# First block's experts: two DRAM accumulators instead of one for the rows that the experts add

## The chip, the cores and the metric

The kernel runs on one core of a Trainium2 chip. The metric is device time in microseconds (us) of one execution. The engines are called PE (TensorE), DVE (VectorE), ACT (ScalarE), POOL (GpSimd) and SP (SyncE); SP computes nothing here and issues the large loads. ACT and POOL issue transfers too, in their own order of work.

## What is computed

Two transformer blocks, one after the other, on 512 tokens of 1024 features. The change lies in the first block's mixture of experts. Each token goes to 8 of 64 experts; its rows are multiplied by a weight and summed, and a shared expert that every token passes is added:

```python
xb = jnp.concatenate([xt, jnp.zeros((1, d), xt.dtype)])[slot_tok].reshape(n_blocks, EXPERT_BLOCK, d)
def expert_block(args):
    xe, e = args
    return (jax.nn.silu(xe @ w_gate_l[e]) * (xe @ w_up_l[e])) @ w_down_l[e]
yb = lax.map(expert_block, (xb, block_e)).reshape(n_slots, d)
routed = jax.ops.segment_sum(yb * slot_w[:, None].astype(yb.dtype), slot_tok, num_segments=t + 1)[:t]
shared = (jax.nn.silu(xt @ w_sh_gate_l) * (xt @ w_sh_up_l)) @ w_sh_down_l
return (routed + shared).reshape(b, l, d)
```

The caller then does `x = x + g2 * _rmsnorm(_moe(h2, *moe_p), norm_ffn_post[i])`, and that `x` is the second block's input.

## The kernel before

`phase_b` holds the first block's expert stage. It works on **blocks**: one block is up to 128 rows (tokens) of one expert. There are 65 blocks of routed experts (128 rows for the first ones, then large and small ones in turn, and at the end of 72 and 64 rows), and ahead of them 4 blocks of the shared expert, one for each 128 tokens. For a routed block the steps are:

- **Gather** (`ex_gather`): POOL issues an indirect DMA that fetches the block's token rows from `h2d` in DRAM into one of four buffers `xg`. So the gather of block b must wait until PE has transposed block b-4.
- **Transpose and two products** (`ex_T`, `ex_gu`): PE transposes `xg`; DVE and ACT copy the result to `xT`; PE multiplies by the gate and up weights (`w`, `wu`); ACT and DVE make `eh`.
- **Down product** (`ex_hT`, `ex_down`): PE multiplies `ehT` by the down weights `wd`; ACT writes the first half of the result `ey`, scaled, and DVE the second half.
- **Scatter** (end of `ex_down`): POOL issues an indirect DMA with an added operation, which adds the rows of `ey` to the rows of `acc`, a [512, 1024] float32 tensor in DRAM. All 65 scatters write the same tensor at places that are known only at run time, so each of them waits on POOL until the one before has landed.

The shared expert's four blocks write `acc` first, as plain DMAs from ACT, and so set its start value.

The weights of an expert are 3 MB: one load `w` of 1 MB and four of 512 KB (`wu`, `wu`, `wd`, `wd`), issued by SP. `wu`, `wd`, `ey`, `xg`, `xT`, the context rows `ct` and the final `ys` are all tiles of 4 KB per partition and share one class of 30 buffers; `u()` hands them out. An instruction that writes such a tile waits for whoever held the buffer before. When that was an `ey`, it waits for a scatter to land.

The code is recorded once, and a scheduler sets each engine's order of instructions. An engine works its list in order: if POOL waits for a landing, the gathers behind wait too.

At the end of the stage stands `overflow()`, a loop whose count is read at run time (for experts that got more rows than planned; it runs no iteration here). All engines meet at its entry and its exit, after all DMAs have landed. Behind it `phase_b` loads `acc` into four tiles `ys` (named `moe` in the trace), and two chains run side by side: PE computes keys and values of the second block's context (`ctx2_kv`, 128 products with `hc`), and `to_mixer` normalizes `ys`, adds it to `x`, normalizes again, and after that PE transposes the result and the second block begins (`hph`, `hpl`). `to_mixer` works on tiles 0 and 1 first, then on 2 and 3.

With 15 blocks to go `ctx2_rows` is started: it loads the context rows `ct` (from ACT), normalizes them (POOL), has PE transpose them and DVE write them to `hc`. Later POOL multiplies a scale `G`.

Of the kernel before, what the change touches and what calls it, by code (L numbers as in the profile page):

```python
# [10 lines left out]
F32 = mybir.dt.float32  # L11
# [10 lines left out]
P = 128  # L22
D = 1024
ND = 8
NX = 512
# [99 lines left out]
class K:  # L125
# [1073 lines left out]
    def phase_b(self):  # L1199
        nc, a, cp, mcol, mT = self.nc, self.a, self.cp, self.mcol, self.mT  # L1200
        self.h2d = self.dp.tile([NX, D], F32, name="h2d")
        self.acc = self.dp.tile([NX, D], F32, name="acc")
        self.x1 = [self.u(D, name="xr") for _ in range(4)]
        for t in range(4):
            nc.scalar.dma_start(self.x1[t], a["x"][t * P:(t + 1) * P])
# [21 lines left out]
        n, nxt, nl = NS + NB, NS + 2, EARLY[0]  # L1227
# [3 lines left out]
        for p in range(n + 1):  # L1231
# [12 lines left out]
            while nl < (EARLY[p] if p < NS else min(NB, b + 1 + AHEAD)):  # L1244
                r, lo, _ = BLOCKS[nl]
# [27 lines left out]
        self.overflow()  # L1273
        wkv += [self.wcols("w_in_2", 1536 + 256 * i, 256) for i in (2, 3)]

        ys = [self.u(D, name="moe") for _ in range(4)]
        for t in range(4):
            nc.sync.dma_start(ys[t], self.acc[t * P:(t + 1) * P])
            self.dump("moe1", ys[t], slice(t * P, t * P + P))
        self.x2 = self.x1  # L1280
        self.hp = []
        self.start(self.to_mixer(ys, G))
# [103 lines left out]
    def route_setup(self):  # L1386
        nc, cp, a = self.nc, self.cp, self.a
        self.wr = self.u(ND, NE, name="wr")
        nc.scalar.dma_start(self.wr, a["w_router"].rearrange("(k p) e -> p k e", p=P))
        shift = self.ps()[:, :NE]  # L1390
        self.acc_mm(shift, [(self.mcol[:, 24 + k:25 + k, 0].to_broadcast([P, P]), self.wr[:, k]) for k in range(ND)])
        self.lsh = self.u(NE, name="lsh1")
        nc.scalar.copy(self.lsh, shift)
        nc.vector.tensor_mul(self.wr, self.wr, self.Af[:, :, None].to_broadcast([P, ND, NE]))
        self.rbias = self.u(NE, name="rbias")
        nc.scalar.dma_start(self.rbias, a["router_bias"].to_broadcast([P, NE]))
        mk = self.mk = self.u(2, P, dt=BF, name="mk")
        nc.vector.tensor_copy(mk[:, 0], self.sq(C_US))
        nc.vector.memset(mk[:, 1], 1.0)
        self.selb = self.u(4, NE, dt=BF, name="selb")  # L1400
        self.pm, self.wts = self.u(4, NE, name="pm"), self.u(4, NE, name="wtsk")

        self.sconst = self.u(4, 3, dt=BF, name="sconst")
        nc.vector.tensor_copy(self.sconst[:, :, 0], self.pos[:, 5:6].to_broadcast([P, 4]))
        for t in range(4):
            nc.vector.memset(self.sconst[:, t, 1:2], float(P * t))
        nc.vector.memset(self.sconst[:, :, 2], 1.0)
        self.aux = self.u(4, NE, 3, dt=BF, name="aux")
        self.iota4 = self.sq(C_IOTA)[:, None, :].to_broadcast([P, 4, P])
        self.cnt = cp.tile([NE, 1], F32, name="cnt")  # L1410
        rr = self.u(2, NE, parts=NE, name="room")
        nc.scalar.dma_start(rr, a["consts"][:NE, O_ROOM:].rearrange("p (r e) -> p r e", r=2))
        self.room, self.rank = rr[:, 0], rr[:, 1]
        self.routed = 0
        self.sorted, self.table = False, {}

    def route(self, t, Ar, Br):
# [131 lines left out]
    def first(self, st):  # L1549

        while self.routed < 4:
            yield
        self.xg = [self.u(D, name="xg") for _ in range(4)]
        for t in range(4):
            self.nc.gpsimd.memset(self.xg[t], 0.0)
        yield from self.slots_steps(0)
        for i in range(2):
            st[NS + i] = self.ex_gather(i)
# [76 lines left out]
    def ex_down(self, s):  # L1635
        nc, c, m = self.nc, s["c"], s["m"]
        y = self.u(D, name="ey")[:c]
        if m == NARROW:
            ps = self.ps()
            for k in range(2):  # L1640
                for j in range(2):
                    nc.tensor.matmul(ps[64 * j:64 * j + 64], s["hT"][:, k], s["wd"][k][:, 512 * j:512 * j + 512],  # L1642
                                     start=(k == 0), stop=(k == 1), tile_position=(0, 64 * j))
            parts = [(ps[64 * j:64 * j + c], s["sw"][64 * j:64 * j + c]) for j in range(2)]
        else:
            parts = []
            for j in range(2):
                ps = self.ps()[:m]
                self.acc_mm(ps, [(s["hT"][:, k], s["wd"][k][:, 512 * j:512 * j + 512]) for k in range(2)])
                parts.append((ps[:c], s["sw"] if "row" in s else s["sw"][:c]))  # L1650
        nc.scalar.activation(y[:, 0:512], parts[0][0], AF.Copy, scale=parts[0][1])
        nc.vector.tensor_scalar(y[:, 512:], parts[1][0], parts[1][1], None, op0=OP.mult)  # L1652
        if "row" in s:
            nc.scalar.dma_start(self.acc[s["row"] * P:(s["row"] + 1) * P], y)
            return
        nc.gpsimd.indirect_dma_start(out=self.acc, out_offset=bass.IndirectOffsetOnAxis(ap=s["idx"][:c], axis=0),  # L1656
                                     in_=y, in_offset=None, bounds_check=NX - 1, oob_is_err=False, compute_op=OP.add)

    def sort_plan(self):
# [699 lines left out]
```

## Time and profile before

| | |
|---|---|
| time, median of 3 runs | 2878.65 us (2872.04 to 2881.9) |
| the profiled execution: its time | 2867.02 us |
| its span, first to last instruction | 2865.2 us |
| mean granted TensorE clock | 0.96 |
| PE busy | 2506.8 us, 87% of the span |
| DVE / ACT / POOL busy | 1064.5 / 541.7 / 588.6 us |
| read and written in DRAM | 748.08 MB and 31.13 MB, 272 GB/s over the span |
| scatters (line 1656 on POOL) | 65, from 797.6 to 1526.7 us |

The times of stages are given as us from the span's start. A busy share says how much an engine worked, not what it was waiting for; for that the rows name in square brackets the idle time ahead of an instruction and what ended it. DMA-issuing instructions on SP and ACT do not count as busy. A DMA's time to landing runs from its issue to its completion.

### The profile page before, as it was taken

What the parts mean: (1) busy time and instruction counts of PE and PEld (TensorE: products, weight loads), DVE (VectorE), ACT (ScalarE), POOL (GpSimd) and SP (SyncE); (2) the same over time, 40 slices, a digit from 0 to 9 for tenths busy, and PEclk for the clock granted to TensorE, in tenths of its full rate; (3) what the DMA queues carried; (4) which work ended last, traced back from release to release, by engine and by line L of the source; (5) the groups of instructions that cost most, each with busy time, mean ns of one, the idle gap of its engine ahead of it and who ended that gap; (6) DMA issues with size and microseconds to landing.
All of it is one profiled execution on the core that took longest, in us unless ns stands there. A gap on an engine that the chain in (4) does not pass through costs nothing. (4 is left out here: it accounts for less than half of the span.)

```text
span 2865.2 us, 36192 instructions
## 1 busy us (share of the span) xinstructions
PE 2506.8 (87%) x13445; PEld 1413.4 (49%) x13445; DVE 1064.5 (37%) x2642; ACT 541.7 (19%) x1129; POOL 588.6 (21%) x438
## 2 busy tenths in 40 slices
PE   6999989998999999887865979969988888888886
PEld 3767869976455443333324858823333333333332
DVE  3673853466434422221213896432111121111122
ACT  4442532122211111111102225300000000000001
POOL 3241343344122112222222652310000000000000
PEclk8999999999999999998987989989999999999998
DMA  7676221145389999999876111389999999999997
GB/s 264 239 267 218 73 82 44 46 144 192 129 309 343 344 342 344 345 332 287 275 221 187 39 60 32 137 312 411 411 411 410 412 412 412 411 411 410 411 411 287
DMA packets 231043, 775.49 MB, mean 271 GB/s; under 512 B 28178, under 2 KB 74450, under 8 KB 207058
## 3 DMA queue, kind: packets, MB, share of 16 engines
q1 hardware_dynamic: 203536, 714.68, 66.0%
q0 software_dynamic: 16288, 37.79, 5.8%
q10 hardware_dynamic: 11042, 20.70, 2.1%
q8 instruction: 107, 1.75, 0.3%
q14 instruction: 70, 0.57, 0.1%
HBM read 748.08 MB, written 31.13 MB: 272 GB/s over the span
## 5 line engine op out<-in xcount | busy, mean ns | idle before, releaser
L2238 PE MATMUL ps<-wu,xT 128*64 128x512 f32 x1448 | 358.6, 596 | 0.1
L2238 PEld LDWEIGHTS ps<-wu,xT 128*64 128x64 f32 x1448 | 129.5, 137 | 210.6 <-issue 185.9
L210 POOL TENSOR_TENSOR wsl<-w,wsh 128x1024 fp32r<-128x1024 f32 x60 | 159.8, 2672 | 236.7 <-ACT wsh L209 192.5
L2293 POOL TENSOR_TENSOR fin<-fin,norm_final_g 128x512 f32<-128x512 f32 x2 | 2.7, 1353 | 984.6 <-ACT fin L2286 984.6
L2244 DVE TENSOR_TENSOR hid<-hid,ps 128x512 f32<-128x512 f32 x32 | 21.4, 687 | 482.7 <-issue 452.7
L2238 PE MATMUL ps<-w,xT 128*64 128x512 f32 x584 | 149.6, 605 | 46.8 <-DMA w<-in_w_up 46.0
L2257 PE MATMUL ps<-wu,hT 128*64 128x512 f32 x752 | 169.1, 594 | 14.1 <-ACT hT L2249 14.1
L1612 PE MATMUL ps<-w,xT 128*128 128x512 f32 (+6 forms) x320 | 153.3, 624 | 27.6 <-DMA w<-in_w_expert 15.3
L1656 POOL DMA_INDIRECT acc<-ey,sidx x65 | 99.0, 1524 | 379.2 <-DMA acc<-ey,sidx 211.9
L1612 PE MATMUL ps<-wu,xT 128*128 128x512 f32 (+6 forms) x320 | 150.4, 610 | 8.4 <-DMA wu<-in_w_expert 4.6
L222 PE MATMUL ps<-wd,ehT 128*128 128x512 f32 (+6 forms) x320 | 145.5, 598 | 1.7 <-DVE ehT L1633 0.9
L1578 POOL DMA_INDIRECT xg<-h2d,sidx x65 | 66.6, 1025 | 234.4 <-PE ps L1642 107.9
L1874 DVE SCALAR_TENSOR_TENSOR cy<-cv,cw,cy 128x512 f32<-128x512 f32 x120 | 114.2, 1013 | 0.4
L1612 PEld LDWEIGHTS ps<-w,xT 128*128 128x128 f32 (+6 forms) x320 | 53.3, 172 | 118.6 <-issue 91.2
L2257 PEld LDWEIGHTS ps<-wu,hT 128*64 128x64 f32 x752 | 53.0, 137 | 116.8 <-issue 93.0
L2238 PEld LDWEIGHTS ps<-w,xT 128*64 128x64 f32 x584 | 43.4, 137 | 136.2 <-issue 68.9
L2243 ACT ACTIVATE hid<-ps 128x512 f32<-128x512 f32 x32 | 18.2, 596 | 481.9 <-PE ps L2238 418.0
L2262 DVE TENSOR_TENSOR y<-ps,G 128x512 f32<-128x512 f32 x16 | 11.1, 692 | 249.0 <-PE ps L2257 249.0
L1612 PEld LDWEIGHTS ps<-wu,xT 128*128 128x128 f32 (+6 forms) x320 | 50.8, 168 | 83.7 <-issue 73.0
L251 PE MATMUL ps<-hxh,wsh 128*128 128x512 f32 x296 | 87.2, 422 | 5.4 <-ACT wsh L209 3.1
L1652 DVE TENSOR_SCALAR ey<-ps,sw 72x512 f32<-72x512 f32 (+6 forms) x65 | 48.7, 749 | 115.9 <-PE ps L222 48.4
L1622 ACT ACTIVATE eh<-ps 128x256 f32<-128x256 f32 (+6 forms) x69 | 23.3, 337 | 358.1 <-PE ps L1612 191.7
(657 smaller groups left out, 4453.2 us busy)
## 6 DMA issues: line engine op xcount, KB each, us to landing
wu<-in_w_down SPq DMA_DIRECT2D x188, 512.0 KB, 11.5
wu<-in_w_up SPq DMA_DIRECT2D x182, 512.0 KB, 11.4
wu<-in_w_gate SPq DMA_DIRECT2D x180, 512.0 KB, 11.4
w<-in_w_expert SPq DMA_DIRECT2D x64, 1024.0 KB, 16.4
wu<-in_w_expert SPq DMA_DIRECT2D x128, 512.0 KB, 14.1
wd<-in_w_expert SPq DMA_DIRECT2D x128, 512.0 KB, 14.6
w<-in_w_mod SPq DMA_DIRECT2D x48, 1024.0 KB, 5.6
w<-in_w_up SPq DMA_DIRECT2D x37, 1024.0 KB, 12.6
```

Source lines behind the costliest of these rows:

```text
L210: (lo or self.nc.vector).tensor_sub(low, x, hi.bitcast(F32))
L222: self.nc.tensor.matmul(ps, l, r, start=(i == 0), stop=(i == n - 1))
L251: self.nc.tensor.matmul(ps, l, r, start=(i == 0), stop=(i == n - 1))
L1578: self.nc.gpsimd.indirect_dma_start(out=self.xg[b % 4][:c], out_offset=None, in_=self.h2d, in_offset=bass.IndirectOffsetOnAxis(ap=idx[:c], ...
L1612: nc.tensor.matmul(ps[:m], x, w[k], start=first, stop=last)
L1622: nc.scalar.activation(hv, v[:, 0], AF.Silu)
L1652: nc.vector.tensor_scalar(y[:, 512:], parts[1][0], parts[1][1], None, op0=OP.mult)
L1656: nc.gpsimd.indirect_dma_start(out=self.acc, out_offset=bass.IndirectOffsetOnAxis(ap=s["idx"][:c], axis=0), in_=y, in_offset=None, bounds_ ...
L1874: nc.vector.scalar_tensor_tensor(y[:, j], vs[j][:, k:k + NX], tap, y[:, j], op0=OP.mult, op1=OP.add)
L2238: nc.tensor.matmul(pgu[gi][c][64 * j:64 * j + 64], xT[:, k], w[j][c], start=(k == 0), stop=(k == ND - 1), tile_position=(0, 64 * j))
L2244: nc.vector.tensor_mul(hid[:, c], hid[:, c], pgu[1][c])
L2257: nc.tensor.matmul(py[64 * j:64 * j + 64], hT[fc][:, ff, 64 * fj:64 * fj + 64], w[r][j], start=(ft == 0), stop=(ft == 15), tile_position=( ...
```

## The change

There are two accumulators in DRAM, `acc` and `acb`. `acc` is set by the shared expert as before; `acb` is set to zero by four DMAs from ACT that copy the freshly zeroed `xg` tiles. The routed scatters take turns (the first goes to `acb`). At the end `acc` is loaded by SP into `moe` and `acb` by ACT into four more tiles `mob`, and four additions (two on DVE, two on POOL) sum them.

```diff
@@ -1199,7 +1199,7 @@
     def phase_b(self):
         nc, a, cp, mcol, mT = self.nc, self.a, self.cp, self.mcol, self.mT
         self.h2d = self.dp.tile([NX, D], F32, name="h2d")
-        self.acc = self.dp.tile([NX, D], F32, name="acc")
+        self.acc = [self.dp.tile([NX, D], F32, name=n) for n in ("acc", "acb")]
         self.x1 = [self.u(D, name="xr") for _ in range(4)]
         for t in range(4):
             nc.scalar.dma_start(self.x1[t], a["x"][t * P:(t + 1) * P])
@@ -1273,10 +1273,14 @@
         self.overflow()
         wkv += [self.wcols("w_in_2", 1536 + 256 * i, 256) for i in (2, 3)]
 
-        ys = [self.u(D, name="moe") for _ in range(4)]
+        ys, zs = [[self.u(D, name=n) for _ in range(4)] for n in ("moe", "mob")]
         for t in range(4):
-            nc.sync.dma_start(ys[t], self.acc[t * P:(t + 1) * P])
+            nc.sync.dma_start(ys[t], self.acc[0][t * P:(t + 1) * P])
+            nc.scalar.dma_start(zs[t], self.acc[1][t * P:(t + 1) * P])
+        for t in range(4):
+            (nc.gpsimd if t % 2 else nc.vector).tensor_add(ys[t], ys[t], zs[t])
             self.dump("moe1", ys[t], slice(t * P, t * P + P))
+        del zs
         self.x2 = self.x1
         self.hp = []
         self.start(self.to_mixer(ys, G))
@@ -1411,7 +1415,7 @@
         rr = self.u(2, NE, parts=NE, name="room")
         nc.scalar.dma_start(rr, a["consts"][:NE, O_ROOM:].rearrange("p (r e) -> p r e", r=2))
         self.room, self.rank = rr[:, 0], rr[:, 1]
-        self.routed = 0
+        self.routed, self.turn = 0, 0
         self.sorted, self.table = False, {}
 
     def route(self, t, Ar, Br):
@@ -1553,6 +1557,7 @@
         self.xg = [self.u(D, name="xg") for _ in range(4)]
         for t in range(4):
             self.nc.gpsimd.memset(self.xg[t], 0.0)
+            self.nc.scalar.dma_start(self.acc[1][t * P:(t + 1) * P], self.xg[t])
         yield from self.slots_steps(0)
         for i in range(2):
             st[NS + i] = self.ex_gather(i)
@@ -1651,9 +1656,10 @@
         nc.scalar.activation(y[:, 0:512], parts[0][0], AF.Copy, scale=parts[0][1])
         nc.vector.tensor_scalar(y[:, 512:], parts[1][0], parts[1][1], None, op0=OP.mult)
         if "row" in s:
-            nc.scalar.dma_start(self.acc[s["row"] * P:(s["row"] + 1) * P], y)
+            nc.scalar.dma_start(self.acc[0][s["row"] * P:(s["row"] + 1) * P], y)
             return
-        nc.gpsimd.indirect_dma_start(out=self.acc, out_offset=bass.IndirectOffsetOnAxis(ap=s["idx"][:c], axis=0),
+        self.turn ^= 1
+        nc.gpsimd.indirect_dma_start(out=self.acc[self.turn], out_offset=bass.IndirectOffsetOnAxis(ap=s["idx"][:c], axis=0),
                                      in_=y, in_offset=None, bounds_check=NX - 1, oob_is_err=False, compute_op=OP.add)
 
     def sort_plan(self):
```

The order of instructions moves with it, above all on POOL. In the rows below a name ends in the number of its tile, the size is that of what is written, and line numbers behind the change stand 5 to 6 higher. The first place is POOL at the context rows (`ct`), at some 1300 to 1345 us of the profile. Before:

```order
L1578 DMA xg_7192<-h2d,sidx_11154 72x1024
L1656 DMA acc<-ey_10499,sidx_10002 512x1024
L1578 DMA xg_7193<-h2d,sidx_11154 64x1024
L1656 DMA acc<-ey_10602,sidx_10002 512x1024
L1656 DMA acc<-ey_10664,sidx_10290 512x1024
L1656 DMA acc<-ey_10725,sidx_10290 512x1024
L1656 DMA acc<-ey_10787,sidx_10290 512x1024
L1812 TENSOR_SCALAR ct_2432_11334<-ct_2432_11334,rs_11426 128x1024
L1812 TENSOR_SCALAR ct_2433_11335<-ct_2433_11335,rs_11426 128x1024
L1656 DMA acc<-ey_10890,sidx_10290 512x1024
L1578 DMA xg_7190<-h2d,sidx_11474 72x1024
L1578 DMA xg_7191<-h2d,sidx_11474 64x1024
```

And now:

```order
L1583 DMA xg_7193<-h2d,sidx_11159 72x1024
L1662 DMA acc<-ey_10730,sidx_10295 512x1024
L1583 DMA xg_7194<-h2d,sidx_11159 64x1024
L1662 DMA acb<-ey_10792,sidx_10295 512x1024
L1662 DMA acc<-ey_10895,sidx_10295 512x1024
L1662 DMA acb<-ey_10957,sidx_10583 512x1024
L1662 DMA acc<-ey_11018,sidx_10583 512x1024
L1818 TENSOR_SCALAR ct_2432_11339<-ct_2432_11339,rs_11431 128x1024
L1818 TENSOR_SCALAR ct_2433_11340<-ct_2433_11340,rs_11431 128x1024
L1583 DMA xg_7191<-h2d,sidx_11479 72x1024
L1583 DMA xg_7192<-h2d,sidx_11479 64x1024
L1583 DMA xg_7193<-h2d,sidx_11479 72x1024
```

Before the change 43 scatters and 56 gathers stand ahead of `ct`, now 46 and 56; the four or five scatters that stand in a row there are now of alternating targets. The second place is POOL at the end of the stage, from the last gather to the read of the loop's count `nX`. Before:

```order
L1578 DMA xg_7190<-h2d,sidx_12058 72x1024
L1656 DMA acc<-ey_11498,sidx_10866 512x1024
L1271 TENSOR_TENSOR G_2612_12095<-G_2612_12095,norm_ffn_post_12093 128x1024
L1656 DMA acc<-ey_11560,sidx_11154 512x1024
L1656 DMA acc<-ey_11655,sidx_11154 512x1024
L1656 DMA acc<-ey_11721,sidx_11154 512x1024
...
L1656 DMA acc<-ey_12261,sidx_11800 512x1024
L1656 DMA acc<-ey_12290,sidx_11800 512x1024
L1656 DMA acc<-ey_12307,sidx_12058 512x1024
L1781 TENSOR_LOAD nX
```

And now:

```order
L1583 DMA xg_7191<-h2d,sidx_12063 72x1024
L1662 DMA acc<-ey_11829,sidx_11159 512x1024
L1662 DMA acb<-ey_11891,sidx_11479 512x1024
L1271 TENSOR_TENSOR G_2612_12100<-G_2612_12100,norm_ffn_post_12098 128x1024
L1662 DMA acc<-ey_11952,sidx_11479 512x1024
L1662 DMA acb<-ey_12014,sidx_11479 512x1024
...
L1662 DMA acb<-ey_12266,sidx_11805 512x1024
L1662 DMA acc<-ey_12295,sidx_11805 512x1024
L1662 DMA acb<-ey_12312,sidx_12063 512x1024
L1787 TENSOR_LOAD nX
```

Behind the last gather 14 scatters stood, 13 of them behind `G`; now 10 do, 8 of them behind `G`. The third place is ACT behind the loop, where `kc` are keys of the context, `junk,ss<-moe` the first sums of squares of `to_mixer`, and `wsh` parts of the second block's weights. Before:

```order
L1829 COPY kc_12463<-ps_12465 128x256
L1302 ACTIVATE junk_12471,ss_12470<-moe_12449 128x1024
L1829 COPY kc_12463<-ps_12533 128x256
L1302 ACTIVATE junk_12473,ss_12470<-moe_12450 128x1024
L1302 ACTIVATE junk_12476,ss_12475<-moe_12451 128x1024
L1829 COPY kc_12463<-ps_12577 128x256
L1302 ACTIVATE junk_12478,ss_12475<-moe_12452 128x1024
L1829 COPY kc_12463<-ps_12587 128x256
```

And now:

```order
L1279 DMA mob_12458<-acb 128x1024
L1279 DMA mob_12459<-acb 128x1024
L1279 DMA mob_12460<-acb 128x1024
L1279 DMA mob_12461<-acb 128x1024
L1835 COPY kc_12480<-ps_12482 128x256
L1835 COPY kc_12480<-ps_12550 128x256
L1306 ACTIVATE junk_12488,ss_12487<-moe_12454 128x1024
L1835 COPY kc_12480<-ps_12594 128x256
L1306 ACTIVATE junk_12490,ss_12487<-moe_12455 128x1024
L1835 COPY kc_12480<-ps_12604 128x256
L1306 ACTIVATE junk_12493,ss_12492<-moe_12456 128x1024
L1840 COPY vc_12481<-ps_12614 128x256
```

Four issues stand ahead now, and each sum of squares comes later among the others, since it waits for an addition.

## Rows read from the trace of the kernel before

**Rows 1.** Windows: start:end, length, busy us (count) of PE, PEld, DVE, ACT, POOL; clock, DMA share, GB/s

```profile
700.00:760.00 60.00, 48.77 (x226) 29.34 (x226) 42.35 (x154) 14.95 (x24) 22.35 (x15) 0.89 0.36 130
...
931.00:1003.00 72.00, 70.39 (x390) 35.02 (x387) 31.16 (x103) 9.01 (x18) 13.35 (x11) 1.00 1.01 343
...
1289.00:1361.00 72.00, 52.25 (x232) 21.82 (x230) 14.27 (x40) 7.98 (x16) 20.38 (x13) 0.85 0.93 287
1361.00:1432.00 71.00, 60.49 (x314) 26.49 (x314) 21.23 (x51) 8.09 (x17) 16.06 (x12) 0.91 0.87 275
1432.00:1486.00 54.00, 44.87 (x153) 16.66 (x153) 9.25 (x27) 6.83 (x14) 11.42 (x8) 0.97 0.86 283
1486.00:1534.00 48.00, 0.47 (x1) 0.47 (x2) 0.28 (x1) 0.00 (x0) 11.51 (x8) 0.54 0.31 43
```

**Rows 2.** Timeline of PE, 1430 to 1640: start, us, line, operation [idle before, what ended it]

```profile
1481.85 3.65 PE L222 MATMUL ps<-wd,ehT 128*72 128x512 f32 x8 [0.93 <-DVE ehT L1633]
1533.53 16.11 PE L251 MATMUL ps<-hc,w 128*128 128x256 f32 x64 [48.03 <-issue]
...
1568.92 5.08 PE L226 MATMUL ps<-cst,moe 128*128 128x128 f32 x32 [5.47 <-DVE rqi L193]
```

**Rows 3.** Waits of all engines, 1486 to 1560: us in total, times, longest

```profile
POOL acc L1656 <- DMA acc<-ey,sidx: 35.1, 8, 5.0
```

**Rows 4.** Timeline of POOL, the last gather and the last scatter

```profile
1428.88 1.03 POOL L1578 DMA_INDIRECT xg<-h2d,sidx  x1 [0.89 <-issue]
...
1526.74 1.48 POOL L1656 DMA_INDIRECT acc<-ey,sidx  x1 [4.72 <-DMA acc<-ey,sidx]
```

**Rows 5.** DMA view, 1490.7 to 1515: busy tenths in 40 slices; scatters, median us to landing

```profile
DMA  0009457300000947600000916651000009773000
...
acc<-ey,sidx POOLq DMA_INDIRECT x5, 5.3
```

**Rows 6.** Waits of all engines, 1290 to 1490

```profile
POOL acc L1656 <- DMA acc<-ey,sidx: 114.0, 16, 16.4
```

**Rows 7.** DMA view, the gather issued at 907.04 and the scatter at 909.71, us to landing

```profile
xg<-h2d,sidx POOLq DMA_INDIRECT x1, 10.3
...
acc<-ey,sidx POOLq DMA_INDIRECT x1, 12.1
```

**Rows 8.** Timeline of PE, 1285 to 1435, its idle times for buffers

```profile
1320.88 6.20 PE L1612 MATMUL ps<-w,xT 128*72 128x512 f32 x8 [8.56 <-DVE xT L1596]
...
1330.79 6.36 PE L1612 MATMUL ps<-wu,xT 128*72 128x512 f32 x8 [3.60 <-ACT xT L1596]
...
1367.32 1.12 PE L226 MATMUL ps<-cst,xg 64*128 64x64 f32 x8 [10.18 <-DVE hc L393]
```

**Rows 9.** Timeline of DVE, same stretch, the copies that PE waited for

```profile
1320.37 0.46 DVE L1596 COPY xT<-ps 128x288 f32<-128x288 f32 x1 [11.15 <-DMA acc<-ey,sidx]
...
1366.72 3.71 DVE L393 TENSOR_SCALAR hc<-ps,Ac,mcol 128x256 f32<-128x256 f32 x8 [10.46 <-DMA acc<-ey,sidx]
```

**Rows 10.** Timeline of ACT, same stretch, the context rows

```profile
1326.16 1.06 ACT L342 ACTIVATE junk<-ct 128x1024 bf16<-128x1024 f32 x1 [17.61 <-DMA ct<-in_ctx]
```

**Rows 11.** Waits of SP's own queue, 1290 to 1490

```profile
SPq L1566 <- DMA acc<-ey,sidx: 42.6, 6, 13.3
```

**Rows 12.** Timeline of ACT and DVE behind the loop

```profile
1543.64 1.06 ACT L1302 ACTIVATE junk<-moe 128x1024 bf16<-128x1024 f32 x1 [3.96 <-DMA moe<-acc]
...
1552.94 1.21 DVE L1310 TENSOR_TENSOR xr<-xr,moe 128x1024 f32<-128x1024 f32 x1
...
1560.65 3.26 DVE L1310 TENSOR_TENSOR xr<-xr,moe 128x1024 f32<-128x1024 f32 x1
```

**Rows 13.** Tile moe, instructions and issues

```profile
L1310 POOL TENSOR_TENSOR xr<-xr,moe x2: 3317/3323/3329, 1549.7 to 1559.5; 128x1024 f32<-128x1024 f32 x2
...
DMA to landing us min/median/max: 9.3/9.5/9.7
```

**Rows 14.** Timeline of POOL at the start of the stage, the first gather

```profile
755.33 1.14 POOL L1578 DMA_INDIRECT xg<-h2d,sidx  x1 [19.21 <-DVE sw L1514]
```

## Prediction

> **What bounds the kernel now.** I read the stage by windows first, then the end of the stage on PE and POOL, then the waits. In the windows [rows 1] three stretches differ. From 931 to 1003 PE is busy throughout and the DMA engines move 343 GB/s at full share: the weight stream and PE are in balance, and nothing that POOL does shows there. From 1289 to 1486 the rate falls to 275 to 287 GB/s and PE's busy share to between 73% and 85%: something holds both. From 1486 to 1534 PE does nothing at all. The timeline of PE [rows 2] gives the edges: the last product of the experts starts at 1481.85, runs 3.65 us and ends at 1485.5, the first product behind the loop starts at 1533.53, after 48.03 us of idle time that the row can only call "issue", because it is spent at the loop's entry, where all engines meet. What POOL does in that time stands in the waits [rows 3]: 8 scatters wait for the scatter before, 35.1 us in all. With 1.48 us for its own issue [rows 4] a scatter takes 35.1/8 + 1.48 = 5.9 us, and the last of them starts at 1526.74 [rows 4], 40 us after the last rows to be added were ready. So the stage does not end with its products but with a queue of scatters.
>
> Why the queue is there is in two more views. In the DMA view of this empty stretch [rows 5] the engines are busy for about 3 us out of each 6 (some five of every ten slices of 0.6 us): half of a scatter's time is latency with nothing moving. Under the weight stream a scatter waits 114.0/16 = 7.1 us for the one before [rows 6], 8.6 us with its issue. And in POOL's order the scatters stand far behind their products: when the last gather is issued, at 1428.88 [rows 4], 14 of them are still to come, 120 us of work at that pace in the 57 us that the stage has left.
>
> **The tail.** The change lets a scatter go when the one before the previous has landed. Two indirect DMAs of POOL do overlap in this trace: the gather issued at 907.04 took 10.3 us and the scatter issued 2.67 us later took 12.1 [rows 7], so they landed 4.5 us apart although each took over 10. Two in flight give one scatter per (7.1 + 1.48)/2 = 4.3 us under load. Behind the last gather 10 scatters are now left instead of 14 (second order shown). 10 x 4.3 = 43 us, with 10 us allowed for `G` among them, which waits for ACT, is 53; the last `ey` is ready at 1486.3, 57 us behind the gather (the end of the last product, and 0.8 us for a copy of 512 columns, by the 0.46 us for 288 in [rows 9]). So the queue should be empty when PE ends. The last scatter then starts at about 1486.6, lands 5.3 us later [rows 5] at 1491.9, and PE follows as it did before, 1533.53 - (1526.74 + 5.3) = 1.5 us later, at 1493.4. That is 40.1 us earlier. One scatter still waiting would cost up to 4.3, and I take half of it off: **-38**. Bounds: nothing waiting, -40. No overlap at all, only the new order: in 57 - 10 us 5.5 of the 10 scatters get done at 8.6 us, the other 4.5 take 5.9 us each, 26.6 us, and PE starts at 1486.3 + 26.6 + 1.5 = 1514.4, -19.
>
> **The stalls from 1289 on.** PE's three idle times there are 8.56, 3.60 and 10.18 us [rows 8]. The first and the third end with a DVE copy that itself waited 11.15 and 10.46 us for a scatter to land [rows 9], since the copy's buffer had held an `ey`. The second waited for ACT, which stood 17.61 us at the context rows [rows 10]; their load needed buffers of the same class, and the scatters that stand in a row ahead of `ct` in the first order shown were under way then, one after the other. Two groups of products beside them took 6.20 and 6.36 us [rows 8], against 3.65 for as many columns in [rows 2], with the clock at 0.85 in that window [rows 1]: 5.3 us more. Together 27.6 us. What is late next is the weight stream. 287 x 72 + 275 x 71 + 283 x 54 is 55.5 MB, at 343 GB/s 162 us instead of 197, so at most 35 us are there; but with fewer stalls PE eats up the weights that were loaded during them and will meet more late loads. I take two thirds of 27.6: **-18**. Bounds: 0, if all of it comes back as waits for weights, and -28.
>
> From 800 to 1289 I count nothing: the bytes are the same and the engines were full.
>
> **The merge.** Behind the loop 2 MB more are read, on ACT's queue beside SP's. Before, ACT starts on the first tile at 1543.64 [rows 12], with 9.5 us from issue to landing [rows 13]. 2.1 MB at 343 GB/s are 6.1 us for the last pair of tiles, about 4 for the first. Then come the additions: one of this size took 1.21 us on DVE and 3.26 when POOL worked beside it [rows 12], and 3.32 on POOL [rows 13]. `to_mixer` needs tile 1 first, which POOL adds: 4 + 3.3 is 7.3 us; tile 3 follows while DVE works on tiles 0 and 1. ACT's sums of squares now stand behind more copies (third order), some 0.7. PE's transposes already wait 5.47 us for this chain [rows 2], so nothing covers it: **+8**. Bounds: 3.3, if the second loads are hidden behind the first, and 14, if loads, both POOL additions and a DVE addition follow each other. The Trainium skill ("SBUF — State Buffer", section "SBUF: two separate sides") says that a DVE operation with two SBUF inputs and a POOL operation exclude each other for their whole length; by it the four additions would stand in line, 9 us, and the merge would be nearer to +12 and the sum to 43. The 1.21 and 3.26 us of [rows 12] agree with it, as far as one pair of rows can; I keep 8, because tile 3 has time.
>
> **The zeroes.** Four issues from ACT and 2.1 MB of writes, 6.1 us of DMA time, in a stretch where the DMA engines are at 0.36 [rows 1]. The first gather, which must not overwrite a tile before its zeroes are out, waits until 755.33 for its indices anyway [rows 14]. What waits behind the issues on ACT is the router's exponential and the stores to `h2d`: **+1**, bounds 0 and 6.
>
> The sum: -38 - 18 + 8 + 1 = -47 us. The profiled execution took 2867.02 us, so 2820. The median of the runs shown is 2878.65, 11.6 us above it; on its footing the forecast is 2878.65 - 47 = **2832 us**.
>
> **Rivals.** *The stalls come back.* The tail closes, but the weights set the pace from 1289 on: -38 + 9 = -29, 2850. For it: the buffers that the weight loads get still come from scatters, and SP waited 42.6 us for them [rows 11]. Against it: at 275 GB/s the stream was not at its limit. Chance 0.16; 0.70 for the forecast, whose own range, with most of each term's bounds, is 2815 to 2848.
>
> *The change does not do what it says.* Both accumulators pass POOL's one DMA queue, and their scatters still land one behind the other. Then only the new order works, -19, the stalls stay, and the merge and the zeroes cost 9: -10, 2869. For it: in the empty stretch the engines are busy half of the time, so that a long scatter could hold the next. Against it: the landings of [rows 7]. The Trainium skill ("DMA: Bandwidth & Descriptors", section "SWDGE vs HWDGE vs iDMA") says that one queue only is allocated to the path that POOL uses; if it meant one transfer at a time, this rival would be the result, and the 4.5 us between two landings speak against that reading. Chance 0.08.
>
> *Slower: the weight stream is held.* The scheduler planned with quicker scatters and gave weight loads buffers of later scatters. If scatters land later than planned, SP, which issues in order, holds all loads behind such a one. It must cost each of the 61 blocks behind the first four 29/61 = 0.48 us to eat the gain of the tail; at 1 us a block it is 61 - 29 = +32, 2911. For it: the waits of SP in [rows 11]. Against it: it needs scatters that are later than before, and they go earlier. Chance 0.06.
>
> **How the numbers follow.** 0.3% of the time, 8.6 us, is about what a measurement of this kernel can tell from no change. The forecast and the first rival are faster by more, the second lies at that edge (half of it), the third is slower: 0.70 + 0.16 + 0.04 = 0.90 faster, 0.04 the same, 0.06 slower. The range takes the forecast with wide terms and the first rival: 2808 to 2858.
>
> **What will show it.** The idle time of PE ahead of the first product with `hc` falls from 48 to some 8 to 12 us; POOL's wait for scatters, 35.1 us there, falls below 10. In the tail two scatters start within 3 us of each other. The waits of DVE for scatters in [rows 9] are gone or short, and the rate from 1289 on is above 300 GB/s. From the first product with `hc` to the first transpose of `moe` it is 35.4 us now and should be 43. I am wrong if scatters to different targets still start 6 us or more apart in the tail, if PE waits for weights about as long as it waited for buffers, or if the stretch from 800 to 1289 grows.

## The result, and the profile after

The changed kernel takes 2828.93 us (median of 4 runs, 2826.22 to 2832.87) against 2875.35 us (4 runs, 2871.92 to 2881.9): ratio 0.9837, 95% interval 0.9813 to 0.9861. The forecast was 2832 us. The profiled execution took 2827.61 us, its span is 2825.8 us.

First the windows of the stage, as in [rows 1]: start and end, length, busy us (count) of PE, PEld, DVE, ACT and POOL, then granted clock, DMA share and GB/s.

```profile
700.00:760.00 60.00, 48.76 (x229) 29.64 (x228) 43.14 (x160) 15.15 (x24) 21.60 (x14) 0.89 0.45 168
931.00:1003.00 72.00, 70.39 (x394) 34.96 (x389) 31.16 (x102) 9.02 (x18) 17.17 (x14) 0.98 1.01 342
1289.00:1361.00 72.00, 58.53 (x268) 24.91 (x268) 19.83 (x50) 8.50 (x18) 20.80 (x13) 0.91 1.01 329
1361.00:1432.00 71.00, 65.32 (x339) 27.99 (x336) 17.94 (x45) 9.40 (x20) 19.12 (x14) 0.98 0.99 324
```

The stretch of 931 to 1003 us is unchanged; from 1289 us on the rate is 329 and 324 GB/s where it was 287 and 275, and PE is busy for 81% and 92% of the time. The timeline of PE at the stage's end (start, us, operation, idle time before it and what ended it) answers to [rows 2]:

```profile
1467.09 3.62 PE L222 MATMUL ps<-wd,ehT 128*72 128x512 f32 x8 [0.45 <-issue]
1479.06 16.57 PE L251 MATMUL ps<-hc,w 128*128 128x256 f32 x64 [8.35 <-issue]
1523.34 6.20 PE L226 MATMUL ps<-cst,moe 128*128 128x128 f32 x32 [13.89 <-DVE rqi L193]
1530.49 4.36 PE L251 MATMUL ps<-hph,wsh 128*128 128x512 f32 x15 [0.95 <-DVE hpr L1340]
```

The last expert product ends at 1470.71 instead of 1485.5, and the idle time ahead of the first `hc` product is 8.35 us instead of 48.03. But PE now waits 13.89 us, not 5.47, for the chain that makes `moe` ready for its transposes. Why the queue is gone stands in POOL's timeline, which answers to [rows 4]:

```profile
1415.88 1.04 POOL L1583 DMA_INDIRECT xg<-h2d,sidx  x1 [0.30 <-issue]
...
1437.67 1.45 POOL L1662 DMA_INDIRECT acc<-ey,sidx  x1 [0.17 <-issue]
1439.43 1.49 POOL L1662 DMA_INDIRECT acb<-ey,sidx  x1 [0.30 <-issue]
...
1465.24 1.46 POOL L1662 DMA_INDIRECT acc<-ey,sidx  x1 [4.72 <-DVE ey L1657]
1472.36 1.48 POOL L1662 DMA_INDIRECT acb<-ey,sidx  x1 [5.66 <-DVEq L1788]
```

Two scatters to the two targets start 1.76 us apart. The last two wait for DVE, no longer for another scatter, where eight waited 35.1 us in [rows 3] (`DVEq L1788` is DVE's own step into the loop, just behind its copy of the last `ey`, which ends at 1471.56). The last one starts at 1472.36 and PE restarts 6.7 us later; of those, 5.4 are its landing. The DMA view of 1437 to 1441 us (median us from issue to landing) shows how much such a pair overlaps:

```profile
acc<-ey,sidx POOLq DMA_INDIRECT x1, 8.8
acb<-ey,sidx POOLq DMA_INDIRECT x1, 9.5
```

One lands at 1437.67 + 8.8 = 1446.5, the other at 1439.43 + 9.5 = 1448.9: 2.5 us apart, though each took about 9. Both went through POOL's one queue. The sentence of the Trainium skill that the second rival drew on ("DMA: Bandwidth & Descriptors", section "SWDGE vs HWDGE vs iDMA": one queue only is allocated) therefore doesn't mean one transfer at a time.

Behind the loop, DVE's and POOL's timelines show the merge and what stands beside it (L1281 is the new addition; L195 and L198 are steps of the reciprocal root on 128x2 elements):

```profile
1493.51 1.23 DVE L1281 TENSOR_TENSOR moe<-moe,mob 128x1024 f32<-128x1024 f32 x1 [21.95 <-DMA moe<-acc]
1494.77 2.36 POOL L1281 TENSOR_TENSOR moe<-moe,mob 128x1024 f32<-128x1024 f32 x1 [20.93 <-DVE moe L1281]
1495.99 2.21 DVE L1281 TENSOR_TENSOR moe<-moe,mob 128x1024 f32<-128x1024 f32 x1 [1.26 <-DMA moe<-acc]
...
1498.75 2.39 POOL L1281 TENSOR_TENSOR moe<-moe,mob 128x1024 f32<-128x1024 f32 x1 [1.63 <-DMA mob<-acb]
1498.95 2.21 DVE L195 TENSOR_TENSOR rqu<-rs 128x2 f32<-128x2 f32 x1
1501.51 2.36 POOL L210 TENSOR_TENSOR wsl<-wa,wsh 128x1024 fp32r<-128x1024 f32 x1 [0.37 <-ACT wsh L209]
1501.58 2.30 DVE L198 TENSOR_TENSOR rqu<-rs 128x2 f32<-128x2 f32 x1
```

The first pair of tiles is added 14.4 us behind the restart of PE (1493.51 - 1479.06), where the first tile alone came 10.1 us behind it before (1543.64 in [rows 12], less 1533.53). An addition takes 1.23 us on DVE alone and 2.21 beside one on POOL, and a step on 128x2 elements takes 2.21 us while POOL adds. The step (L195) ends at 1501.16, just behind POOL's addition, which ends at 1501.14; the second addition on DVE ends 1.07 us behind POOL's first, about the time that it takes alone.

### The profile page after: what moved, and what is told of

It reads as the page before. It is cut to its first block, busy times and chain, and to the rows that moved or that the text cites. A ratio compares the mean times of both kernels' runs of the same rounds, so it can differ in the third digit from the quotient of the medians.

```text
span 2825.8 us, 36213 instructions
## 1 busy us (share of the span) xinstructions
PE 2514.5 (89%) x13445; PEld 1416.6 (50%) x13445; DVE 1071.7 (38%) x2644; ACT 542.3 (19%) x1129; POOL 594.0 (21%) x440
## 5 line engine op out<-in xcount | busy, mean ns | idle before, releaser
L2244 PEld LDWEIGHTS ps<-w,xT 128*64 128x64 f32 x584 | 42.6, 137 | 139.7 <-issue 69.8
L1662 POOL DMA_INDIRECT acb<-ey,sidx x33 | 52.7, 1596 | 167.7 <-DVE ey L1657 79.5
L222 PEld LDWEIGHTS ps<-wd,ehT 128*128 128x128 f32 (+6 forms) x320 | 50.5, 168 | 73.2 <-issue 61.4
## 6 DMA issues: line engine op xcount, KB each, us to landing
wd<-in_w_expert SPq DMA_DIRECT2D x128, 512.0 KB, 14.6
```

The lines of the kernel that those rows point to most:

```text
L222: self.nc.tensor.matmul(ps, l, r, start=(i == 0), stop=(i == n - 1))
L1662: nc.gpsimd.indirect_dma_start(out=self.acc[self.turn], out_offset=bass.IndirectOffsetOnAxis(ap=s["idx"][:c], axis=0), in_=y, in_offset=No ...
L2244: nc.tensor.matmul(pgu[gi][c][64 * j:64 * j + 64], xT[:, k], w[j][c], start=(k == 0), stop=(k == ND - 1), tile_position=(0, 64 * j))
```

## Experiments

Each ratio is against the kernel before, run beside it. That kernel took 2865.66 to 2897.26 us in the runs beside these, with medians from 2871.27 to 2878.39 us, so a few us between the medians of two rows, or between two single profiles, say nothing. Three columns are read from PE's timeline: the end of the last expert product, the idle time ahead of the first `hc` product, and the time from that product to the first one with `hph`, which holds the merge; the fourth is from there to the end of the span. The traces count 65 routed blocks, where two of the expectations say 64.

| kernel | last product ends | idle | `hc` to `hph` | `hph` to end | median us | ratio (95%) |
|---|---|---|---|---|---|---|
| before | 1485.5 | 48.03 | 41.42 | 1290.3 | 2875.35 | |
| changed | 1470.7 | 8.35 | 51.43 | 1295.3 | 2828.93 | 0.9837 (0.9813 to 0.9861) |
| one target | 1484.2 | 45.25 | 51.52 | 1297.1 | 2887.47 | 1.0047 (1.0024 to 1.0071) |
| first 33 alternate | 1489.4 | 48.13 | 51.02 | 1302.5 | 2892.16 | 1.0044 (1.0013 to 1.0075) |
| first 49 alternate | 1470.0 | 44.25 | 51.77 | 1293.6 | 2863.75 | 0.9956 (0.9927 to 0.9984) |
| same, early load | 1482.0 | 37.28 | 46.88 | 1291.1 | 2865.19 | 0.9963 (0.9939 to 0.9987) |
| last 32 alternate | 1472.3 | 35.92 | 50.27 | 1293.4 | 2859.19 | 0.9956 (0.9930 to 0.9982) |
| last 16 alternate | 1469.2 | 38.88 | 51.28 | 1294.8 | 2854.64 | 0.9913 (0.9887 to 0.9939) |
| three targets | 1478.2 | 3.73 | 52.80 | 1308.4 | 2838.77 | 0.9868 (0.9810 to 0.9925) |
| no merge | 1469.8 | 8.61 | 41.85 | 1289.4 | 2815.73 | 0.9790 (0.9772 to 0.9808) |
| additions on DVE | 1473.2 | 8.30 | 49.59 | 1302.4 | 2829.74 | 0.9827 (0.9810 to 0.9843) |
| tiles first | 1470.0 | 8.15 | 51.58 | 1298.5 | 2828.85 | 0.9834 (0.9776 to 0.9891) |
| `ct` on ACT | 1468.5 | 8.08 | 51.52 | 1298.4 | 2828.58 | 0.9834 (0.9777 to 0.9891) |
| both small edits | 1472.9 | 8.19 | 49.65 | 1302.4 | 2840.83 | 0.9894 (0.9875 to 0.9913) |

And a second table, for the runs that differ in how the targets are used: the blocks whose rows are ready (second half of `ey` started on DVE, the four that are stored by row left out) and whose scatter has not started, at three times, counted in the timelines of DVE and POOL.

| kernel | 1100 us | 1289 us | 1432 us |
|---|---|---|---|
| before | 9 | 10 | 9 |
| one target | 11 | 10 | 9 |
| first 33 alternate | 2 | 10 | 8 |
| first 49 alternate | 3 | 7 | 7 |
| last 32 alternate | 10 | 9 | 7 |
| last 16 alternate | 10 | 10 | 6 |
| changed | 3 | 6 | 4 |
| three targets | 0 | 0 | 0 |

**One target.**

```diff
-        self.turn ^= 1
```

> Every routed scatter adds to the first accumulator, the second is still zeroed, loaded and added. The order of the instructions is that of the changed kernel but for what the scheduler moves with the slower scatters. Theory (the alternation gives the gain): tail and stalls are back as before and the merge and the zeroes are still paid, 2875 + 11 = about 2886 us, PE idle ahead of the first product with hc about 48 us, scatters 6 us apart in the tail. Rival (the new order gives most of it): 2860 us or less, idle below 30 us.

The theory holds: 2887.47 us, idle 45.25 us, and the last eight scatters start 4.7 to 6.3 us apart again. What the change costs without its benefit is 0.47%, 13.5 us; in the profiles 10.1 us of it lie between `hc` and `hph`, and the span ends 12.9 us later in all. The two windows from 1289 us on move 288 and 289 GB/s, and SP's weight loads wait 46.3 us for scatters (42.6 in [rows 11]). PE's rows at the stage's end:

```profile
1480.58 3.65 PE L222 MATMUL ps<-wd,ehT 128*72 128x512 f32 x8 [0.93 <-DVE ehT L1638]
1529.48 17.00 PE L251 MATMUL ps<-hc,w 128*128 128x256 f32 x64 [45.25 <-issue]
```

So the stalls hang on the alternation too. But POOL's order went back with it: 43 scatters stand ahead of `ct` and 14 behind the last gather again, as before the change. The run therefore shows what the second target brings together with the order that it allows; the overlap without that order, or the order without the overlap, was not run.

**The last 16 blocks.**

```diff
-        self.turn ^= 1
+        if s["b"] >= 49:
+            self.turn ^= 1
...
```

(`b` is the block's number, which one more changed line hands on.)

> The targets alternate only for the last 16 of the 64 routed blocks, the others add to the first accumulator. Theory A (what counts is the pace of the last scatters): the tail is closed, idle ahead of the first product with hc 8 to 12 us, and the stalls from 1289 us on are gone too, 2829 to 2836 us. Theory B (the stalls are cured by the pace of the scatters in the middle of the stage): tail closed, stalls back, 2829 + 17 = about 2846 us. If the backlog built in the first three quarters is too long for the last one, the idle time stays above 20 us and the time is above 2845.

The third case came out, 2854.64 us and an idle time of 38.88 us. The stalls are cured, the last product ending at 1469.2, and no stall over 4.5 us is left between 1289 and 1435 us, although 43 scatters stand ahead of `ct` as before; SP's weight loads wait 8.1 us for scatters from 1290 to 1490 us, where they waited 42.6 and, with one target, 46.3. The tail is not: the last eight scatters in POOL's timeline are

```profile
1463.35 1.49 POOL L1663 DMA_INDIRECT acb<-ey,sidx  x1 [14.04 <-DVE ey L1657]
1465.14 1.48 POOL L1663 DMA_INDIRECT acc<-ey,sidx  x1 [0.30 <-issue]
1472.14 1.47 POOL L1663 DMA_INDIRECT acc<-ey,sidx  x1 [5.52 <-DMA acc<-ey,sidx]
1477.83 1.48 POOL L1663 DMA_INDIRECT acc<-ey,sidx  x1 [4.21 <-DMA acc<-ey,sidx]
1483.55 1.47 POOL L1663 DMA_INDIRECT acc<-ey,sidx  x1 [4.24 <-DMA acc<-ey,sidx]
1489.39 1.48 POOL L1663 DMA_INDIRECT acc<-ey,sidx  x1 [4.37 <-DMA acc<-ey,sidx]
1495.11 1.47 POOL L1663 DMA_INDIRECT acc<-ey,sidx  x1 [4.25 <-DMA acc<-ey,sidx]
1501.39 1.48 POOL L1663 DMA_INDIRECT acc<-ey,sidx  x1 [4.81 <-DMA acc<-ey,sidx]
```

Seven scatters to the first target stand in a row, 5.7 to 7.0 us apart: the arrears of the blocks before. Those to the second target went ahead of them.

**The last 32 blocks.** The same edit with 33 for 49.

> The targets alternate for the last 32 of the 64 routed blocks. Theory (a backlog of scatters to the first accumulator, built up while they go one at a time, is what stood in the tail of the run with the last 16): twice as many blocks alternate, the backlog is worked off before the end, idle ahead of the first product with hc 8 to 12 us, 2829 to 2834 us. Rival (the scatters to one target must be alternated from the start): idle of 20 us or more, 2842 us or more.

The theory was wrong: twice the blocks change nothing in the tail (35.92 us, 2859.19 us). The arrears fall only from 10 to 7 between 1100 and 1432 us. POOL's timeline shows one reason:

```profile
1450.75 1.84 POOL L1663 DMA_INDIRECT acc<-ey,sidx  x1 [4.43 <-DMA acc<-ey,sidx]
1464.82 1.49 POOL L1663 DMA_INDIRECT acb<-ey,sidx  x1 [12.23 <-DVE ey L1657]
1466.61 1.49 POOL L1663 DMA_INDIRECT acc<-ey,sidx  x1 [0.31 <-issue]
```

POOL issues in order, and in this order a scatter to the second target stands ahead of seven to the first. It waits 12.23 us for rows that aren't ready, while those seven, most of them with their rows ready, stand behind it. Such waits for rows of the second target add up to 43.2 us in 9 places between 1100 and 1510 us.

**The first 33 and the first 49 blocks**, with 33 and with 49 in this line (and `b` handed on as above).

```diff
-        self.turn ^= 1
+        self.turn = 1 - self.turn if s["b"] < 33 else 0
```

> The targets alternate for the first 33 of the 65 routed blocks, the rest add to the first accumulator. Counted in the traces, at 1100 us 11 blocks are ready and not yet scattered in the kernel with one target used, 10 in the run with the last half alternated, 3 in the changed kernel, and these numbers hardly change up to 1432 us. Theory (the backlog that forms before 1100 us is what stands in the tail): the backlog stays below 6, idle ahead of the first product with hc below 20 us, 2830 to 2842 us. Rival (one target cannot follow the second half either): idle above 30 us, 2850 us or more.

> The targets alternate for the first 49 of the 65 routed blocks. Theory as for the first half: backlog below 6 at 1432 us, idle 8 to 15 us, 2828 to 2838 us. Rival: the last 16 blocks alone, one at a time, bring back a queue in the tail, idle above 25 us and 2845 us or more.

Both rivals came out, and with them falls the theory that the backlog of the first third is what stands in the tail. After 33 alternating blocks 2 are in arrears at 1100 us, but 10 at 1289 us and 48.13 us of idle time at the end; SP waits 48.9 us for scatters between 1290 and 1490 us, and the stalls are there in full. With 49 the arrears stay near those of the changed kernel until 1400 us, the last product ends as early as there, and then 14 scatters to one target, the first at 1404.58 and the last at 1507.69, start 103.1/13 = 7.9 us apart on average (6.5 from 1435.99 on, where nearly all of them wait for the one before): 44.25 us idle. So, in the orders that the scheduler made, the second target had to be in use both while the blocks come quickly and behind the last gather; each of the four parts alone leaves 35.9 us or more of the 48. The stalls are another matter. The last product ends at 1469 to 1472 us with the first 49, the last 32 and the last 16 blocks, and SP's weight loads wait 14.6, 3.3 and 8.1 us for scatters in these; with the first 33 it ends at 1489.4. Why such different parts cure the stalls stays open.

**The merge left out.**

```diff
-            nc.scalar.dma_start(zs[t], self.acc[1][t * P:(t + 1) * P])
...
-            (nc.gpsimd if t % 2 else nc.vector).tensor_add(ys[t], ys[t], zs[t])
```

> The scatters alternate as in the changed kernel, but the second accumulator is neither loaded nor added at the end, so its rows are missing from what follows; it is there to price the merge. Theory: the first product with hc to the first product with hph is 10 us shorter, the time is 2829 - 10 = 2819 us. Rival (part of the 10 us is covered by ACT's sums of squares and by the load of the first tiles, or is given back later): 2824 or more.

The merge is worth 2828.93 - 2815.73 = 13.2 us by the medians, 13.5 by the ratios. In the profiles, 16.1 us apart, 9.6 lie between `hc` and `hph`, as expected, and 5.9 behind that. The rival, a cheaper merge, is excluded.

**All additions on DVE.**

```diff
-            (nc.gpsimd if t % 2 else nc.vector).tensor_add(ys[t], ys[t], zs[t])
+            nc.vector.tensor_add(ys[t], ys[t], zs[t])
```

> All four additions at the end of the stage stand on DVE, none on POOL. Theory (additions on POOL and DVE lengthen each other and the steps of the norm beside them): four additions of 1.2 us in line instead of pairs of 2.2 to 2.4, and DVE's short steps of the norm at 0.1 to 0.2 us instead of 2.2, first transpose of moe 3 to 4 us earlier, about 2825 us. Rival (the additions were not what ends last, the loads are): the first transpose moves by less than 1 us, 2829 us. Either difference is near what the comparison can tell, so the rows decide.

The steps behave as the theory has it. DVE's timeline:

```profile
1495.76 2.44 DVE L1281 TENSOR_TENSOR moe<-moe,mob 128x1024 f32<-128x1024 f32 x2 [21.68 <-DMA moe<-acc]
...
1501.13 0.16 DVE L195 TENSOR_TENSOR rqu<-rs 128x2 f32<-128x2 f32 x1
...
1501.72 0.16 DVE L198 TENSOR_TENSOR rqu<-rs 128x2 f32<-128x2 f32 x1
1501.99 1.22 DVE L1281 TENSOR_TENSOR moe<-moe,mob 128x1024 f32<-128x1024 f32 x1
...
1503.72 3.49 DVE L1313 SCALAR_TENSOR_TENSOR moe<-moe,rs,G 128x1024 f32<-128x1024 f32 x1
```

Two additions take 2.44 us together, and the short steps 0.16 us. The first scaled tile (L1313) starts 22.2 us behind the first `hc` product instead of 25.7. But then it runs beside POOL's `wsl` and takes 3.49 us, and the first transpose is only 1.4 us nearer to the restart; the time, 2829.74 us, is that of the rival. The Trainium skill ("SBUF — State Buffer", section "SBUF: two separate sides") says that a DVE operation with two SBUF inputs and a POOL operation that reads SBUF exclude each other; 1.23 us against 2.21 for the same addition, and 0.16 against 2.21 for a short step, agree with it. Moving the additions off POOL gives little back here: the stretch from `hc` to `hph` still takes 49.59 us, 8.2 more than before the change.

**The tiles' loads first.**

```diff
-        wkv += [self.wcols("w_in_2", 1536 + 256 * i, 256) for i in (2, 3)]
...
             nc.scalar.dma_start(zs[t], self.acc[1][t * P:(t + 1) * P])
+        wkv += [self.wcols("w_in_2", 1536 + 256 * i, 256) for i in (2, 3)]
```

> Behind the loop the eight loads of the two accumulators are issued ahead of the last two context weight loads (2 MB) instead of behind them. Theory (the merge ends last on the landing of its tiles, 14.4 us behind the restart of PE): 2 MB at about 390 GB/s are 5 us, so the first addition starts 9 to 10 us behind the first product with hc, the first transpose of moe about 39 us behind it instead of 44.3, and the time is about 2824 us. Rival (the products with the late weights then wait just as long, or the chain of the norm is held elsewhere): transposes at 43 us or more, 2828 or more.

2828.85 us, with the first transpose 44.3 us behind the first `hc` product, as in the changed kernel. The edit moved less than was meant: SP issued one tile of `moe`, then both weight loads, then the other three tiles, so only the first addition came earlier (5.8 us behind the first `hc` product). What all eight loads ahead of the weights would bring stays open.

**The context rows on ACT.**

```diff
-            nc.gpsimd.tensor_scalar(ct[t], ct[t], rs[:, t:t + 1], None, op0=OP.mult)
+            nc.scalar.activation(ct[t], ct[t], AF.Copy, scale=rs[:, t:t + 1])
```

> The two multiplies of the context rows stand on ACT instead of POOL, which held POOL's scatters for 25 us in the middle of the stage. Theory (the stalls that are left from 1289 us on come from that hold): last expert product 4 to 8 us earlier, 2821 to 2825 us. Rival (the weight stream, at 311 to 329 GB/s against 340 before, has hardly anything to give): less than 3 us either way, 2826 to 2832 us.

2828.58 us, the rival's time, but not its reason: the gap in POOL's scatters is still there, 34.1 us instead of 36.8 in the changed kernel. POOL now stands at a gather, for PE:

```profile
1309.23 1.45 POOL L1662 DMA_INDIRECT acc<-ey,sidx  x1 [0.93 <-issue]
1338.86 1.04 POOL L1583 DMA_INDIRECT xg<-h2d,sidx  x1 [28.17 <-PE ps L226]
...
1343.28 1.86 POOL L1662 DMA_INDIRECT acb<-ey,sidx  x1 [0.30 <-issue]
```

The multiplies alone were therefore not what made the gap; what it costs wasn't tried.

**Three targets.**

```diff
-        self.acc = [self.dp.tile([NX, D], F32, name=n) for n in ("acc", "acb")]
+        self.acc = [self.dp.tile([NX, D], F32, name=n) for n in ("acc", "acb", "acd")]
...
-        self.turn ^= 1
+        self.turn = (self.turn + 1) % 3
```

> Three accumulators in turn; the third is zeroed too, but is neither loaded nor added at the end, so its rows are missing from what follows. Theory (with two targets the scatters no longer set the pace): last expert product within 3 us of the kernel with two, zeroes +1, 2827 to 2832 us. Rival (the waits of 19 us for scatters that are left, and the waits of SP for their buffers, still cost time): 2820 us or less.

No scatter is in arrears at any of the three times, and still the last product ends 7.5 us later and the time is 2838.77 us. Having no arrears at all thus brings nothing over two targets here. The idle time of 3.73 us can't be compared with the others, as two rows show:

```profile
1481.97 17.12 PE L251 MATMUL ps<-hc,w 128*128 128x256 f32 x64 [3.73 <-issue]
1482.92 1.49 POOL L1663 DMA_INDIRECT acd<-ey,sidx  x1 [6.33 <-DVE ey L1658]
```

PE restarts before the last scatter to the third accumulator is issued. Nothing reads that accumulator, and its last scatter stands behind the loop in POOL's order; the meeting at the loop waits only for the transfers that were issued ahead of it, not for all. By the medians the kernel is 9.8 us slower, though the intervals of the two ratios overlap. In its profile, the slowest of its four runs, the first `hph` product comes 4.3 us later and the stretch behind it is 13.1 us longer; why was not found.

**The second accumulator loaded early.** As with 49 alternating blocks, and:

```diff
             if p == n - 5:
...
+                zs = [self.u(D, name="mob") for _ in range(4)]
+                for t in range(4):
+                    nc.scalar.dma_start(zs[t], self.acc[1][t * P:(t + 1) * P])
```

> As the run with the first 49 blocks alternated, and the second accumulator, complete by then, is loaded inside the stage, five blocks ahead of its end; only the additions stay behind the loop. Theory (the second loads cost 4 us behind the restart): the first transpose of moe comes some 40 us behind the first product with hc instead of 44, 4 us below that run. Rival (the 2.1 MB then cost 6 us of the weight stream, and four buffers of a row's size are held): 0 to 4 us above it.

The loads behind the restart do cost 51.77 - 46.88 = 4.9 us, but inside the stage they are given back: the last product ends 12.0 us later, and the first `hc` product starts at 1519.33 instead of 1514.29. Whether the bytes or the four buffers held cost it was not separated. 2865.19 against 2863.75 us, the rival.

**Both small edits together**, the additions on DVE and the context rows on ACT.

> The two small edits together: all four additions on DVE, the multiplies of the context rows on ACT. Singly each left the time where it was (2829.7 and 2828.6 us against 2828.9), though one brought the first transpose of moe 1.4 us nearer to the restart and the other the last expert product 2.5 us earlier. Theory (the two small shifts add up): 2825 us. Rival (both are given back behind the merge, where the stretch from the first product with hph to the end took 1289 to 1308 us in the profiles so far): 2828 to 2831 us.

Neither came out: 2840.83 us, slower than either alone. Its profiled execution is the fastest of its four runs (2834.9 us) and has the same stretch behind `hph` as that with the additions on DVE, 1302.4 us; what the other runs lost was not found. No version that gives all rows beats the changed kernel by more than 0.4 us, far less than its own runs differ by.

## Why the prediction was right, and where its terms were off

By the profiled executions the change is worth 39.4 us, by the medians 46.4, and the forecast was 47. From the profiles:

- *The tail, -38:* 48.03 to 8.35 us, **-39.7**, the bound of an empty queue. Behind the last gather 10 scatters were left, as counted; from 1418.16 to 1472.36 they took 54 us where the sum had 53. That agreement is luck, for the last two waited for their rows, so the 54 us are set by the products and not by the pace of 4.3 us. And the step was incomplete: it took the pace behind the last gather for the whole reason, and the runs with the last 16 and 32 blocks show that the arrears must be spread over both targets before that.
- *The other bound, no overlap and only the new order, -19:* not tested, nor the second rival's 2869 us, which rests on it. With one target the first `hc` product starts only 4.0 us earlier (1529.48 against 1533.53), but there the order went back too. What speaks against the second rival is the landings, 2.5 us apart in the tail of the changed kernel.
- *The stalls, -18:* the last product ends 14.8 us earlier although the first scatter starts 1.1 us later, so the stretch between them is shorter by **15.9**. That is the forecast's -18 and its nothing for 800 to 1289 us in one, and how it divides at 1289 us can't be read: the 52nd `ey` copy of DVE, that of the 48th routed block, starts 2.2 us later than before (1284.13 against 1281.9), the one before it 3.1 us earlier, the 54th 9.7 us later. Against the first rival, little of it came back as waits for weights: the longest idle times of PE from 1289 to 1435 us are 3.36, 3.15, 3.31 and 3.56 us, against 8.56, 3.60 and 10.18 in [rows 8]. The first two are for weights. The last is for a DVE copy that still waited for a scatter, 6.14 us where [rows 9] had 11.15 and 10.46:

```profile
1370.69 0.46 DVE L1601 COPY xT<-ps 128x288 f32<-128x288 f32 x1 [6.14 <-DMA acc<-ey,sidx]
```

- *The zeroes, +1:* the first scatter starts at 798.72 instead of 797.65, **+1.1**.
- *The merge, +8:* **+10.0** up to the first `hph` product, 51.43 against 41.42 us; up to the first transpose of `moe` it is 44.27 us, where 43 was foretold. The rule of the Trainium skill on DVE and POOL, put at +12, and the 8 that was chosen lie on either side. The run without the merge confirms the size; the terms in it were the late first pair (4.3 us), and for the rest the additions themselves and DVE operations held up by POOL's; how that rest divides isn't shown, but all additions on DVE gave back only 1.8 us (49.59 against 51.43).
- *Behind the merge nothing was counted,* and the profile is **5.1 us** longer there. That can't be put down to the merge, since kernels that all have it take 1291 to 1308 us for this stretch, in one profile each.

-39.7 - 15.9 + 1.1 + 10.0 + 5.1 = -39.4 us. So the mechanism was right in the tail, the stalls and the merge, and from profile to profile the gain was overestimated by 7.6 us: 2820 was worked out and 2827.6 measured, mainly for the stretch behind the merge. That the median came within 3 us of 2832 is in part luck. The profiled execution of the kernel before, 2867.02 us, was faster than all four of its timed runs (2871.92 us and up), that of the changed kernel only 1.3 us below its median, and so the medians lie 7 us further apart than the profiles. The third rival is excluded: the waits of SP's weight loads for scatters fell from 42.6 us [rows 11] to 22.1 (21.7 for `acb`, 0.4 for `acc`).

## What to carry to other kernels

Where each accumulating scatter to a target waits for the one before to land, as here, what counts is landing, not moved bytes: a second target is worth its zeroing and its merge when scatters are still in a row as the products end. Use it over the whole stage: here none of the parts tried closed the tail, for arrears that belong to one target stay with it, and an engine that issues in order puts new work ahead of them. Price the merge by the first pair of tiles and the engines that add, and read the stretch behind it as well, since it differed by up to 19 us between profiles of kernels that run the same products there; with one profile of each, kernel and execution can't be told apart.

## What was not expected of the hardware

The granted clock of PE falls to its lower level, 1.2 GHz, for about 7 us in the attention stretch of the changed kernel, though PE works there as it did before. The windows of the changed kernel (columns as above, the clock is the third from the end):

```profile
1715.00:1725.00 10.00, 9.15 (x64) 7.45 (x62) 8.30 (x32) 4.98 (x12) 2.77 (x4) 1.00 0.02 4
...
1727.00:1733.00 6.00, 6.00 (x25) 5.05 (x24) 2.09 (x5) 0.59 (x1) 2.06 (x3) 0.50 0.01 3
```

and of the kernel before, where the same products stand:

```profile
1759.00:1769.00 10.00, 9.09 (x63) 7.38 (x62) 8.30 (x32) 5.05 (x12) 2.77 (x4) 1.00 0.03 7
...
1771.00:1777.00 6.00, 5.99 (x40) 4.67 (x39) 4.12 (x7) 2.61 (x6) 2.03 (x3) 1.00 0.02 4
```

25 products instead of 40 in 6 us of unbroken work, behind the same idle time of 0.94 us. In 8 of the 14 profiles the fall is there, near the same products, and in 6 (before, no merge, tiles first, last 32, `ct` on ACT, early load) it isn't. At half the clock for 6.8 us it holds PE back by some 3.4 us, an estimate that can be a part of the 5.1 us behind the merge; but `ct` on ACT, without the fall, is 3.1 us longer there than the changed kernel. What decides it stays open: kernels with and without it have the merge, and both kinds have the alternation.
